# Reading the decay rows back from DRAM on all partitions in place of broadcasting them by matmul

## The chip, the cores and the metric

The kernel runs on one core of a Trainium2 chip. The metric is the device time of one execution in microseconds; the lower, the better.

## The reference

Two blocks run one after the other on a sequence of 256 positions with 1024 channels, each with two layers. A layer of the first block is a feed-forward part, a mixer of three branches (a convolution, a state-space head group, a sparse attention) and another feed-forward part, with layer norms and a modulation. A layer of the second block is a mixer of two branches (a sliding-window attention and a matrix-memory cell) and a feed-forward part.

What matters here are the two places where a decay between two positions is applied. In the state-space branch there are 16 heads in 4 groups, and for each head

```
a_cs = cumsum(a)                                # a < 0, one value for each position
seg[l, s] = exp(a_cs[l] - a_cs[s])  for l >= s, else 0
y = (C B^T * seg) (x dt)
```

In the matrix-memory branch there are 4 heads; with the input and forget gates brought to a running sum b and a running maximum, the same form appears:

```
w[l, s] = exp(b[l] - b[s] + log_i[s] - m[l]) (q_l . k_s)  for l >= s, else 0
```

In both, the exponent is a value of the column minus a value of the row, and for l >= s it is never above zero.

## The kernel before

The sequence is two tiles of 128 positions. Weights come from DRAM in pieces of 128x1024 (512 KB) on SyncE's queue; each piece is split into a high and a low part (ScalarE makes the high part at L187, VectorE the low part at L188), up to four pieces ahead. A unit is one piece with its matmuls: gemm_w (L284 to L286) does three products for each of eight channel tiles, 24 matmuls of 256 columns; gemm_x (L297 to L299) does the same with the operands exchanged, 512 columns. The program is a list of units with small actions between them. Everything that isn't a plain projection runs as a generator beside the units ("side"): after each unit step_sides advances every side by its rate, so the products of attention, convolution and heads are dealt out among the units. The convolution (conv_side, L1204) goes at a fixed number of VectorE instructions for each unit. The instruction order on each engine is fixed when the kernel is built, from the program order and the dependencies; an engine then executes its instructions in that order, and a wait holds all that stands behind it on that engine.

In the first mixer small_project computes the running sum acs for 16 heads as 16 rows of 256 positions, and to_rows turns it into columns. ssd_side takes the four groups: when a group's convolved inputs are there, one step computes the product of B and C (causal_pairs, L924 and L925, with a 0/1 mask at L928 and L929) and turns the inputs; then one step for each head calls decay and, for the head before it, decayed_sum (L934 to L936). In the second mixer mlstm_gates makes the rows and mlstm_side does the same for four heads, with causal_pairs in the same step as decay.

decay needs the row of a head on all 128 partitions, and gets it by a product: split_row has split the row into a high and a low part (tile ahl), and a one-hot column of identr picks head h and spreads it over the partitions, in two matmuls of 384 columns (L911, L912). Two further matmuls add the mask, which is minus 1e30 above the diagonal, to the two diagonal blocks (L913, L914). ScalarE then reads the sum from PSUM, adds the column value as a bias and takes the exponential (L916 with 256 elements, L917 with 128), and VectorE multiplies by the product of B and C (L918).

Of the kernel before, what the change touches and what calls it, by code (L numbers as in the profile page):

```python
# [19 lines left out]
P = 128  # L20
T = 256
# [84 lines left out]
def net_kernel(ctx, tc, a, out, dbg=None):  # L106
# [30 lines left out]
    def f(ap):  # L137
        return ap.bitcast(F32)
# [13 lines left out]
    adb = const.tile([P, DEPTH, 72], F32, name="adb")  # L152
    lncols = const.tile([P, DEPTH, 48], F32, name="lncols")
    ident = cst[:, C_ID:C_ID + P]
    identr = const.tile([P, 16], F32R, name="identr")
    V.tensor_copy(identr, ident[:, 0:16])
    ones = const.tile([P, T], F32, name="ones")
    V.memset(ones, 1.0)
    mhalf = const.tile([P, 8], F32, name="mhalf")
    V.memset(mhalf, -0.5)  # L160
    masks = const.tile([P, 4, P], BF16, name="masks")
    identb, caus_b, strict_b, tcaus_b = (masks[:, i] for i in range(4))

    def load_constants():
        late_load(lncols, a["lncol"])
        late_load(cst[:, P:], a["consts"][:, P:])
        for i, c0 in enumerate((C_ID, C_CAUS, C_STRICT, C_TCAUS)):
            V.tensor_copy(masks[:, i], cst[:, c0:c0 + P])

    def cos_t(tt, n):  # L170
# [710 lines left out]
                yield  # L881
        yield u

    def split_row(x, pp):

        t = rt("ahl", 2 * (T + P), 1, F32R).rearrange("p (a c) -> p a c", a=2)
        hi, lo = t[0:pp, 0], t[0:pp, 1]
        S.activation(hi[:, 0:T], x, AF.Copy)
        V.tensor_sub(lo[:, 0:T], x, f(hi[:, 0:T]))
        V.tensor_copy(t[0:pp, :, T:], f(t[0:pp, :, P:T]))  # L890
        return hi, lo

    def to_rows(stk):
        rows = rt("smrow", 2 * P, 1).rearrange("p (a c) -> p a c", a=2)
# [9 lines left out]
        it = iter([t[:, i * T:(i + 1) * T] for t in ts for i in range(4)])  # L904
        return lambda: next(it)

    def decay(h, hl, nh, brow, cbm):

        sp = tp_tile()[:, :T + P]
        sel = identr[0:nh, h:h + 1].to_broadcast([nh, P])  # L910
        E.matmul(sp, sel, hl[0], start=True, stop=False)  # L911
        E.matmul(sp, sel, hl[1], start=False, stop=False)  # L912
        E.matmul(sp[:, 0:P], identb, tcaus_b, start=False, stop=False)  # L913
        E.matmul(sp[:, T:T + P], identb, tcaus_b, start=False, stop=True)  # L914
        sg = rt("seg", T + P, 2)
        S.activation(sg[:, 0:T], sp[:, 0:T], AF.Exp, bias=brow[:, 0])  # L916
        S.activation(sg[:, T:], sp[:, T:], AF.Exp, bias=brow[:, 1])  # L917
        V.tensor_mul(sg, sg, cbm)  # L918
        return sg

# [124 lines left out]
    def small_project(l, st, ps):  # L1045

        pc = pcols[l]
        al = quarters()
        stk, gt = al(), al()
        G.memset(stk, 0.0)  # L1050
        it = S.activation(gt[64:112], ps[64:112, :T], AF.Tanh, scale=0.5)
        V.tensor_scalar(stk[64:112], gt[64:112], 0.5, 0.5, op0=ALU.mult, op1=ALU.add)
        x = gt[0:16]
        S.activation(x, ps[0:16, :T], AF.Identity, bias=pc[0:16, PC_DTB:PC_DTB + 1])
        for lp in softplus_log(x, 16, al):
            yield
        V.scalar_tensor_tensor(stk[0:16], x, 0.0, lp, op0=ALU.max, op1=ALU.add)
        an = small.tile([P, 1], F32, tag="an", name="an")
        with behind([it]):
            S.activation(an[0:16], pc[0:16, PC_ALG:PC_ALG + 1], AF.Exp)  # L1060
        da, acs = al()[0:16], al()[0:16]
        V.tensor_scalar(da, stk[0:16], an[0:16], -1.0, op0=ALU.mult, op1=ALU.mult)
        V.tensor_tensor_scan(acs, ones[0:16], da, 0.0, op0=ALU.mult, op1=ALU.add)
        S.activation(stk[32:48], acs, AF.Copy, scale=-1.0)
        st["hl"] = split_row(acs, 16)
        yield
        st["rows"] = to_rows(stk)
        yield
# [230 lines left out]
    def ssd_side(l, st):  # L1299
        dsk = small.tile([P, 16], F32, tag="dsk", name="dsk")  # L1300
        late_load(dsk, a["dskip"][l:l + 1].to_broadcast([P, 16]))
        yrow = row_pair()
        st["yrow"] = yrow
        for g in range(4):
            while ("xs", g) not in st:
                yield
            bcT, xg = st["bc", g], st["xs", g]
            rows, hl = st["rows"], st["hl"]
            cbm = causal_pairs(bcT[:, 0:T], bcT[:, T:])
            xdt = rt("xdt", 512, 1).rearrange("p (a h d) -> p a h d", a=2, d=HD)  # L1310
            hs, cs = slice(4 * g, 4 * g + 4), slice(g * T, (g + 1) * T)
            tp = tp_tile()
            for tt in range(2):
                for j in range(2):
                    E.transpose(tp[:, tsl(2 * tt + j)], xg[:, j * T + tt * P:j * T + (tt + 1) * P], ident)
            for tt in range(2):
                tv = tp[:, tt * T:(tt + 1) * T].rearrange("p (h d) -> p h d", d=HD)
                V.tensor_mul(xdt[:, tt], tv, bc(rows[:, tt, hs], HD))
                V.tensor_mul(yrow[tt][:, cs].rearrange("p (h d) -> p h d", d=HD), tv, bc(dsk[:, hs], HD))
            st["ssd_in"] = g + 1  # L1320
            yield
            prev = None
            for r in range(5):
                sg = decay(4 * g + r, hl, 16, rows[:, :, 32 + 4 * g + r:33 + 4 * g + r], cbm) if r < 4 else None
                if prev is not None:
                    yv = tp_tile()[:, :P].rearrange("p (a c) -> p a c", a=2)
                    decayed_sum(yv, prev, lambda tt: xdt[:, tt, r - 1])
                    for tt in range(2):
                        ys = yrow[tt][:, (4 * g + r - 1) * HD:(4 * g + r) * HD]
                        V.tensor_add(ys, ys, yv[:, tt])  # L1330
                prev = sg
                yield
            st["ssd"] = g + 1
# [236 lines left out]
    def mlstm_gates(l, st, ps):  # L1570

        gb, gf = (qcols[l][0:4, QC_GB + j:QC_GB + j + 1] for j in range(2))
        area = bt("ca", 2 * D)
        cuts = iter(range(8))

        def al():
            i = next(cuts) * T
            return area[:, i:i + T]
        stk, ix, fx = al(), al()[0:4], al()[0:4]
        G.memset(stk, 0.0)  # L1580
        S.activation(ix, ps[0:4, :T], AF.Identity, bias=gb)
        S.activation(fx, ps[0:4, T:], AF.Identity, bias=gf)
        for lp in softplus_log(fx, 4, al):
            yield

        V.scalar_tensor_tensor(lp, fx, 0.0, lp, op0=ALU.min, op1=ALU.subtract)
        bs, mx = al()[0:4], al()[0:4]
        V.tensor_tensor_scan(bs, ones[0:4], lp, 0.0, op0=ALU.mult, op1=ALU.add)
        V.tensor_sub(stk[0:4], ix, bs)
        V.tensor_tensor_scan(mx, ones[0:4], stk[0:4], 0.0, op0=ALU.mult, op1=ALU.max)  # L1590
        V.tensor_add(bs, bs, mx)
        S.activation(stk[32:36], bs, AF.Exp, scale=-1.0)
        V.tensor_scalar(mx, mx, -1.0, None, op0=ALU.mult)
        st["hl"] = split_row(mx, 4)
        yield
        yield
        st["rows"] = to_rows(stk)
        yield
# [30 lines left out]

    def mlstm_side(l, st, xm):  # L1630
        hm = row_pair()
        qk, vm, rows, hl, so = st["qk"], st["vm"], st["rows"], st["hl"], st["so"]
        prev = None
        for h in range(5):
            sg = None
            if h < 4:
                pb = (h % 2) * HD
                cbm = causal_pairs(qk[pb:pb + HD, 2 + h // 2], qk[pb:pb + HD, h // 2])
                sg = decay(h, hl, 4, rows[:, :, h:h + 1], cbm)
            if prev is not None:  # L1640
                yield
                p = h - 1
                yp = tp_tile()[:, :260].rearrange("p (a c) -> p a c", a=2)
                decayed_sum(yp, prev, lambda tt: vm[:, tt, p])
                hs = tsl(p)
                den = small.tile([P, 2], F32, tag="den", name="den")
                ss = small.tile([P, 2], F32, tag="mss", name="mss")
                sq = rt("t1", T, 4)
                S.activation(den, yp[:, :, P], AF.Abs)
                V.tensor_max(den, den, rows[:, :, 32 + p])  # L1650
                V.reciprocal(den, den)
                for tt in range(2):
                    V.tensor_scalar(hm[tt][:, hs], yp[:, tt, 0:P], den[:, tt:tt + 1], None, op0=ALU.mult)
                    S.activation(sq[:, 0:P], hm[tt][:, hs], AF.Square, accum_out=ss[:, tt:tt + 1])
                rsqrt_col(ss, ss, 1.0 / P, 1e-6)
                yield
                for tt in range(2):
                    V.scalar_tensor_tensor(hm[tt][:, hs], hm[tt][:, hs], ss[:, tt:tt + 1], so[:, tt, hs],
                                           op0=ALU.mult, op1=ALU.mult)
            prev = sg  # L1660
            yield
# [513 lines left out]
```

## Time and profile before

| what | value |
|---|---|
| median of 3 runs | 2551.43 us (2548.42 to 2554.11) |
| profiled execution | 2554.82 us, span 2552.7 us |
| TensorE, matmuls busy | 2438.5 us, 96% of the span |
| VectorE busy | 1839.7 us, 72% |
| ScalarE busy | 1344.2 us, 53% |
| mean granted TensorE clock | 0.985 of full speed |

The span runs from the first to the last instruction of one profiled execution; that execution's own time is 2.1 us longer and 3.4 us above the median of the runs. PE is TensorE, PEld its weight load, DVE is VectorE, ACT is ScalarE, SP is SyncE; an engine's name with a q is its queue of instructions (DMA issues, semaphores). Busy times count instructions that overlap once. A row of a stretch gives its limits and length, then the busy us (and instructions) of PE, PEld, DVE, ACT and POOL in it. A line number is that of the instruction or of the helper that issued it.

### The profile page before, as it was taken

The page shows a single profiled execution, that of the slowest core. Times are in us where ns is not written, and L with a number is a line of the kernel's source. Part 1 is how long each engine was busy: PE and PEld are TensorE (multiplying, and loading weights), DVE is VectorE, ACT ScalarE, POOL GpSimd, SP SyncE. Part 2 cuts the span into 40 slices and gives each one's busy share as a digit, 9 for nine tenths or more (in the row PEclk, how much of TensorE's full clock was granted, in tenths as well). Part 3 has the DMA queues.
Part 4 walks back from the last instruction along what each step waited for, and adds up shares of the span by engine and source line. Part 5 has one row for each costly group of instructions (what it writes and reads, how often), then busy time and mean ns, then how long its engine had stood idle before and what let it go on. Part 6 is the DMA issues. An engine that isn't in the chain of part 4 may idle for free.

```text
span 2552.7 us, 42530 instructions
## 1 busy us (share of the span) xinstructions
PE 2438.5 (96%) x16604; PEld 2208.8 (87%) x16604; DVE 1839.7 (72%) x3270; ACT 1344.2 (53%) x2356; POOL 69.8 (3%) x128
## 2 busy tenths in 40 slices
PE   8999999989889989989999999999899999999999
PEld 6887889889878879978898999899789898789888
DVE  7768988899786676768988996655766555656554
ACT  5444666544543444435666546545465555555554
POOL 0000000000000000000000000000100000100000
PEclk9999999999999999989999999999999999999999
DMA  9886622256868868875522357457335456436454
GB/s 332 286 301 226 217 101 92 91 171 216 270 218 279 272 205 275 273 242 173 166 67 84 117 188 231 143 189 250 119 121 185 156 187 223 134 100 223 141 187 143
DMA packets 134218, 484.73 MB, mean 190 GB/s; under 512 B 15569, under 2 KB 16129, under 8 KB 134018
## 3 DMA queue, kind: packets, MB, share of 16 engines
q1 hardware_dynamic: 133442, 480.83, 57.0%
q8 instruction: 130, 2.13, 0.3%
q10 hardware_dynamic: 576, 1.19, 0.1%
q14 instruction: 70, 0.57, 0.1%
HBM read 476.69 MB, written 5.27 MB: 189 GB/s over the span
## 4 chain that ended last, share of the span: by engine, by line
PE 61%; DMA 15%; DVE 13%; ACT 5%; issue 4%; POOL 1%; SPq 0%; ACTq 0%; DVEq 0%; POOLq 0%
PE mm L284 10%; PE mm L285 10%; PE mm L286 10%; DMA ada<-in_adaw_dram 8%; PE y L297 6%; PE y L298 6%; PE y L299 6%; DVE lo L188 4%; DVE ca L1204 2%; PE tp L989 2%; ACT hi L187 2%; DMA raw<-in_wg_dram 2%; DVE ada L492 1%; PE tp L980 1%; DMA raw<-in_wo_dram 1%
## 5 line engine op out<-in xcount | busy, mean ns | idle before, releaser
L187 ACT ACTIVATE hi<-raw 128x1024 fp32r<-128x1024 f32 (+1 forms) x676 | 712.6, 1058 | 725.1 <-PE mm L285 367.2
L188 DVE TENSOR_TENSOR lo<-raw,hi 128x1024 fp32r<-128x1024 f32 (+1 forms) x676 | 822.2, 1221 | 304.7 <-ACT hi L187 300.9
L284 PE MATMUL mm<-xTh,hi 128*128 128x256 f32 x2896 | 827.8, 286 | 10.3 <-ACT av L1222 3.0
L286 PE MATMUL mm<-xTh,lo 128*128 128x256 f32 x2896 | 824.2, 285 | 6.5 <-DVE lo L188 6.5
L285 PE MATMUL mm<-xTl,hi 128*128 128x256 f32 x2896 | 822.5, 284 | 2.4 <-DVE xTl L455 2.4
L284 PEld LDWEIGHTS mm<-xTh,hi 128*128 128x128 f32 x2896 | 551.2, 190 | 15.9 <-ACT av L1222 3.7
L286 PEld LDWEIGHTS mm<-xTh,lo 128*128 128x128 f32 x2896 | 550.8, 190 | 9.6 <-DVE lo L188 9.0
L285 PEld LDWEIGHTS mm<-xTl,hi 128*128 128x128 f32 x2896 | 550.7, 190 | 6.5 <-DVE xTl L455 3.2
L299 PE MATMUL y<-hi,q 128*128 128x512 f32 x664 | 264.5, 399 | 1.0 <-DVE q L702 1.0
L492 DVE SCALAR_TENSOR_TENSOR ada<-ada,crow 128x1024 f32<-128x1024 f32 x128 | 156.1, 1221 | 120.7 <-DMA ada<-in_adaw_dram 120.5
L297 PE MATMUL y<-hi,q 128*128 128x512 f32 x552 | 221.8, 402 | 14.2 <-ACT q L701 14.2
L298 PE MATMUL y<-lo,q 128*128 128x512 f32 x552 | 220.7, 400 | 5.0 <-DVE lo L188 5.0
L1204 DVE SCALAR_TENSOR_TENSOR ca<-av,pcol,ca 128x244 f32<-128x244 f32 (+26 forms) x480 | 207.3, 461 | 0.3
L299 PEld LDWEIGHTS y<-hi,q 128*128 128x128 f32 x664 | 126.4, 190 | 32.4 <-DVE q L702 2.0
L297 PEld LDWEIGHTS y<-hi,q 128*128 128x128 f32 x552 | 105.3, 191 | 39.0 <-ACT q L701 16.6
L298 PEld LDWEIGHTS y<-lo,q 128*128 128x128 f32 x552 | 104.9, 190 | 29.5 <-DVE lo L188 7.5
L297 PE MATMUL y<-hi,xTh 128*128 128x512 f32 (+1 forms) x288 | 114.1, 396 | 3.1 <-DVE e8b L830 1.5
L284 PE MATMUL mm<-xyh,hi 128*128 128x256 f32 x384 | 112.2, 293 | 4.2 <-ACT t2d L1366 4.2
L285 PE MATMUL mm<-xyl,hi 128*128 128x256 f32 x384 | 111.7, 291 | 4.4 <-DVE xyl L415 4.4
L286 PE MATMUL mm<-xyh,lo 128*128 128x256 f32 x384 | 111.1, 290 | 0.8 <-DVE lo L188 0.8
L299 PE MATMUL y<-hi,xTl 128*128 128x512 f32 (+1 forms) x288 | 111.1, 386 | 0.0
L298 PE MATMUL y<-lo,xTh 128*128 128x512 f32 (+1 forms) x288 | 110.7, 384 | 0.0
(492 smaller groups left out, 3730.5 us busy)
## 6 DMA issues: line engine op xcount, KB each, us to landing
ada<-in_adaw_dram SPq DMA_DIRECT2D x128, 512.0 KB, 5.2
raw<-in_ff_dram SPq DMA_DIRECT2D x128, 512.0 KB, 4.6
raw<-in_wg_dram SPq DMA_DIRECT2D x88, 512.0 KB, 5.6
raw<-in_wu_dram SPq DMA_DIRECT2D x88, 512.0 KB, 5.6
raw<-in_wd_dram SPq DMA_DIRECT2D x88, 512.0 KB, 5.4
raw<-in_wG_dram SPq DMA_DIRECT2D x48, 512.0 KB, 4.2
raw<-in_wkv_dram SPq DMA_DIRECT2D x16, 512.0 KB, 4.6
raw<-in_wval_dram SPq DMA_DIRECT2D x16, 512.0 KB, 4.3
```

The lines of the kernel that those rows point to most:

```text
L187: S.activation(hi, raw, AF.Copy)
L188: eng.tensor_tensor(lo, raw, f(hi), op=ALU.subtract)
L284: E.matmul(ps, wh[:, wk + k], xh, start=(k == 0), stop=False)
L285: E.matmul(ps, wh[:, wk + k], xl, start=False, stop=False)
L286: E.matmul(ps, wl[:, wk + k], xh, start=False, stop=(k == nk - 1))
L297: return [E.matmul(ps, xh, wh[:, kk, cs], start=first, stop=False), E.matmul(ps, xh, wl[:, kk, cs], start=False, stop=False), E.matmul(ps, ...
L298: E.matmul(ps, xh, wl[:, kk, cs], start=False, stop=False),
L299: E.matmul(ps, xl, wh[:, kk, cs], start=False, stop=last)]
L492: V.scalar_tensor_tensor(raw, raw, 1.0, crow, op0=ALU.mult, op1=ALU.mult, accum_out=col[:, k:k + 1])
L980: E.transpose(tp[:, tsl(r * nbr + b)], pr[:, r, b, tsl(kt)], ident)
L989: E.matmul(o[:, i * HD:(i + 1) * HD], pTs[kt][:, tsl(i)], vof(i % nbr, kt), start=(kt == 0), stop=(kt == tt))
L1204: V.scalar_tensor_tensor(ca[:, k, s:T], av[:, 0:T - s], caw[:, k, w:w + 1], ca[:, k, s:T], op0=ALU.mult, op1=ALU.add)
```

## The change

The one-hot, the split of the row and the four matmuls go. The rows are written to a DRAM tile by a DMA on ScalarE's queue (keep_rows, once in each layer of each mixer), and each head's row of 256 positions is read back on all 128 partitions by another DMA on that queue (decay_rows, two heads in a tile of 2 x 256, three such tiles). In the first mixer all four reads of a group are issued at the start of its step; in the second mixer all four at the start of the side, with a yield behind them. decay then works from SBUF: two Relu of the difference of column and row (on ScalarE, with scale -1 and the column as bias) make it zero where it would be negative, which is only above the diagonal, and one Exp with scale -1 over all 384 elements follows. The 0/1 mask in the product of B and C takes out what is above the diagonal. The columns change sign accordingly.

```diff
-    identr = const.tile([P, 16], F32R, name="identr")
-    V.tensor_copy(identr, ident[:, 0:16])
...
-    masks = const.tile([P, 4, P], BF16, name="masks")
-    identb, caus_b, strict_b, tcaus_b = (masks[:, i] for i in range(4))
+    masks = const.tile([P, 3, P], BF16, name="masks")
+    identb, caus_b, strict_b = (masks[:, i] for i in range(3))
...
-    def split_row(x, pp):
-
-        t = rt("ahl", 2 * (T + P), 1, F32R).rearrange("p (a c) -> p a c", a=2)
-        hi, lo = t[0:pp, 0], t[0:pp, 1]
-        S.activation(hi[:, 0:T], x, AF.Copy)
-        V.tensor_sub(lo[:, 0:T], x, f(hi[:, 0:T]))
-        V.tensor_copy(t[0:pp, :, T:], f(t[0:pp, :, P:T]))
-        return hi, lo
+    decd = [dram.tile([16, T], F32, name="decd%d" % i) for i in range(4)]
+
+    def keep_rows(st, x, i):
+        st["dec"] = decd[i][0:x.shape[0]]
+        S.dma_start(st["dec"], x)
+
+    def decay_rows(st, h):
+
+        t = rt("dec", 2 * T, 3)
+        for j in range(2):
+            S.dma_start(t[:, j * T:(j + 1) * T], st["dec"][h + j:h + j + 1].to_broadcast([P, T]))
+        st["dec", h], st["dec", h + 1] = t[:, 0:T], t[:, T:]
...
-    def decay(h, hl, nh, brow, cbm):
-
-        sp = tp_tile()[:, :T + P]
-        sel = identr[0:nh, h:h + 1].to_broadcast([nh, P])
-        E.matmul(sp, sel, hl[0], start=True, stop=False)
-        E.matmul(sp, sel, hl[1], start=False, stop=False)
-        E.matmul(sp[:, 0:P], identb, tcaus_b, start=False, stop=False)
-        E.matmul(sp[:, T:T + P], identb, tcaus_b, start=False, stop=True)
+    def decay(row, brow, cbm):
+
+
         sg = rt("seg", T + P, 2)
-        S.activation(sg[:, 0:T], sp[:, 0:T], AF.Exp, bias=brow[:, 0])
-        S.activation(sg[:, T:], sp[:, T:], AF.Exp, bias=brow[:, 1])
+        S.activation(sg[:, 0:T], row, AF.Relu, scale=-1.0, bias=brow[:, 0])
+        S.activation(sg[:, T:], row[:, P:T], AF.Relu, scale=-1.0, bias=brow[:, 1])
+        S.activation(sg, sg, AF.Exp, scale=-1.0)
         V.tensor_mul(sg, sg, cbm)
         return sg
...
-        S.activation(stk[32:48], acs, AF.Copy, scale=-1.0)
-        st["hl"] = split_row(acs, 16)
+        S.activation(stk[32:48], acs, AF.Copy)
+        keep_rows(st, acs, l)
...
+            for j in range(0, 4, 2):
+                decay_rows(st, 4 * g + j)
             cbm = causal_pairs(bcT[:, 0:T], bcT[:, T:])
...
-        V.tensor_sub(stk[0:4], ix, bs)
-        V.tensor_tensor_scan(mx, ones[0:4], stk[0:4], 0.0, op0=ALU.mult, op1=ALU.max)
+        V.tensor_sub(ix, ix, bs)
+        V.tensor_scalar(stk[0:4], ix, -1.0, None, op0=ALU.mult)
+        V.tensor_tensor_scan(mx, ones[0:4], ix, 0.0, op0=ALU.mult, op1=ALU.max)
...
-        st["hl"] = split_row(mx, 4)
+        keep_rows(st, mx, DEPTH + l)
...
+        for j in range(0, 4, 2):
+            decay_rows(st, j)
+        yield
```

## Rows read from the trace of the kernel before

**Rows 1.** The page, busy us of the engines, share of the span, instructions.
```profile
PE 2438.5 (96%) x16604; PEld 2208.8 (87%) x16604; DVE 1839.7 (72%) x3270; ACT 1344.2 (53%) x2356; POOL 69.8 (3%) x128
```

**Rows 2.** Busy time by stretch; the last columns are granted clock, DMA share, GB/s.
```profile
340.00:500.00 160.00, 159.67 (x1212) 143.78 (x1210) 130.42 (x370) 103.43 (x283) 9.98 (x26) 0.99 0.27 88
1262.00:1420.00 158.00, 157.41 (x1204) 141.52 (x1203) 129.99 (x379) 102.70 (x282) 12.67 (x28) 1.00 0.24 78
1862.00:1912.00 50.00, 49.95 (x367) 44.84 (x366) 30.02 (x84) 28.65 (x81) 1.87 (x4) 1.00 0.39 121
...
530.00:600.00 70.00, 60.29 (x452) 58.66 (x451) 66.70 (x133) 27.60 (x44) 1.42 (x2) 0.90 0.51 166
```
**Rows 3.** The chain that ended last from 340 to 500 us, by line.
```profile
by line: PE mm L284 12.3%; PE mm L286 12.2%; PE mm L285 12.1%; PE tp L989 10.5%; PE tp L980 4.9%; PE tp L1075 4.6%; PE tp L911 3.7%; PE y L946 3.5%; PE y L947 3.4%; PE tp L867 2.8%; PE y L950 2.3%; PE tp L934 2.3%; PE tp L935 2.2%; PE tp L9
```

**Rows 4.** ACT's waits from 340 to 500 us: us in total, times, longest.
```profile
ACT seg L916 <- PE tp L914: 15.1, 11, 4.1
```

**Rows 5.** Instruction groups of ACT by shape: count, busy us, mean ns, idle before.
```profile
L454 ACT ACTIVATE xTh<-t 128x256 fp32r<-128x256 f32 x72 | 28.9, 417 | 2.1 <-DVE t L446 1.1 <-DVE t L448 0.4
...
L916 ACT ACTIVATE seg<-tp,smrow 128x256 f32<-128x256 f32 x40 | 19.0, 475 | 30.6 <-PE tp L914 30.4
...
L917 ACT ACTIVATE seg<-tp,smrow 128x128 f32<-128x128 f32 x40 | 14.6, 365 | 0.0
...
L1286 ACT ACTIVATE sac<-sac 128x512 f32<-128x512 f32 x16 | 10.2, 635 | 0.3
...
L1201 ACT ACTIVATE ca<-av,pcol 128x256 f32<-128x256 f32 x16 | 8.7, 594 | 0.2
```

**Rows 6.** PE in order of time around one decay set: start us, us, instruction.
```profile
361.89 0.28 PE L284 MATMUL mm<-xTh,hi 128*128 128x256 f32 x1
362.10 0.43 PE L911 MATMUL tp<-ahl,identr 16*128 16x384 f32 x1
362.38 0.33 PE L912 MATMUL tp<-ahl,identr 16*128 16x384 f32 x1
362.64 0.23 PE L913 MATMUL tp<-masks 128*128 128x128 bf16 x1
362.71 0.22 PE L914 MATMUL tp<-masks 128*128 128x128 bf16 x1
362.74 0.37 PE L285 MATMUL mm<-xTl,hi 128*128 128x256 f32 x1
362.94 0.28 PE L286 MATMUL mm<-xTh,lo 128*128 128x256 f32 x1
363.06 0.28 PE L284 MATMUL mm<-xTh,hi 128*128 128x256 f32 x1
```

**Rows 7.** Single lines on ACT: ns min/median/max, first and last start.
```profile
L875 ACT ACT_TABLE_LOAD  x1: 1283/1283/1283, 1839.9 to 1839.9; - x1
...
L819 ACT ACTIVATE t2d<-mm x32: 575/580/598, 2000.2 to 2537.6; 128x512 f32<-128x512 f32 x32
...
L964 ACT ACTIVATE t<-y,aneg x160: 348/424/504, 355.8 to 2287.9; 128x128 f32<-128x128 f32 x80, 128x256 f32<-128x256 f32 x80
```

**Rows 8.** A DMA issue of ACT (the inputs' load): ns min/median/max, starts.
```profile
L1786 ACTq DMA_DIRECT2D row<-in_x_dram x2: 452/452/453, 1.1 to 1.6; - x2
```

**Rows 9.** Who waited for whom in the whole span: us in total, times, longest.
```profile
ACT seg L916 <- PE tp L914: 30.4, 25, 4.1
```

**Rows 10.** PE in order of time, from a group's products to its first decay.
```profile
1379.72 0.59 PE L924 MATMUL tp<-sac 128*128 128x256 f32 x2
...
1385.13 0.43 PE L911 MATMUL tp<-ahl,identr 16*128 16x384 f32 x1
```

**Rows 11.** DMA issues: count, KB each, median us to landing.
```profile
cst<-in_consts_dram ACTq DMA_DIRECT2D x1, 64.0 KB, 2.0
```

**Rows 12.** The late loads on SP's queue, L238: ns of an issue, and landing.
```profile
L238 SPq DMA_DIRECT2D row<-hd x8: 372/424/1348, 654.5 to 2323.0; - x8
...
DMA to landing us min/median/max: 5.0/6.8/9.9
```

More of the change, by code (lines that the diff above doesn't have):

```diff
@@ L166, in load_constants @@
         late_load(cst[:, P:], a["consts"][:, P:])
-        for i, c0 in enumerate((C_ID, C_CAUS, C_STRICT, C_TCAUS)):
+        for i, c0 in enumerate((C_ID, C_CAUS, C_STRICT)):
             V.tensor_copy(masks[:, i], cst[:, c0:c0 + P])
@@ L1307, in ssd_side @@
             bcT, xg = st["bc", g], st["xs", g]
-            rows, hl = st["rows"], st["hl"]
+            rows = st["rows"]
+            for j in range(0, 4, 2):
+                decay_rows(st, 4 * g + j)
             cbm = causal_pairs(bcT[:, 0:T], bcT[:, T:])
@@ L1323, in ssd_side @@
             for r in range(5):
-                sg = decay(4 * g + r, hl, 16, rows[:, :, 32 + 4 * g + r:33 + 4 * g + r], cbm) if r < 4 else None
+                h = 4 * g + r
+                sg = decay(st["dec", h], rows[:, :, 32 + h:33 + h], cbm) if r < 4 else None
                 if prev is not None:
@@ L1631, in mlstm_side @@
         hm = row_pair()
-        qk, vm, rows, hl, so = st["qk"], st["vm"], st["rows"], st["hl"], st["so"]
+        qk, vm, rows, so = st["qk"], st["vm"], st["rows"], st["so"]
+        for j in range(0, 4, 2):
+            decay_rows(st, j)
+        yield
         prev = None
@@ L1638, in mlstm_side @@
                 cbm = causal_pairs(qk[pb:pb + HD, 2 + h // 2], qk[pb:pb + HD, h // 2])
-                sg = decay(h, hl, 4, rows[:, :, h:h + 1], cbm)
+                sg = decay(st["dec", h], rows[:, :, h:h + 1], cbm)
             if prev is not None:
```

## Prediction

> **What bounds the kernel now.** I read the page's busy times first [rows 1]: TensorE (PE) is busy 96% of the span, VectorE (DVE) 72%, ScalarE (ACT) 53%. That is an average, so next I read the busy times of the stretches in which the decay products run [rows 2]. The reader is to see that PE has nothing left there: 159.67 us of 160 in the first mixer of layer 0, 157.41 of 158 in layer 1, 49.95 of 50 in the second mixer's stretch (its other layer reads the same), with DVE at 130 us of 160 and ACT at 103. The last line of that group is the stretch behind: there DVE is at 66.70 of 70 and PE at 60.29. The chain of waits in the first stretch [rows 3] runs through PE matmuls, with the first product of the change (L911) taking 3.7% of it. The list of waits [rows 4] shows the other side: ACT stood idle 15.1 us in that stretch only because the last decay product (L914) was not done. So in these stretches PE issues without a hole, and an instruction taken from it should come off the time.
>
> **What is removed from PE.** decay() runs 40 times: 16 heads in each of two layers, 4 in each of two (the count in [rows 5]). Each run has four matmuls: two of 384 columns (the row's high and low part against the one-hot) and two 128x128 masks. A PE row's own duration includes its pipeline, so I go by starts [rows 6]: L911 starts at 362.10 and the next foreign matmul at 362.74, so a set holds PE for 0.64 us. The spacing of two plain matmuls is 363.06 - 362.94 = 0.12; at the two seams it is 0.21 (361.89 to 362.10) and 0.20 (362.74 to 362.94), so the seams add up to 0.09 + 0.08 = 0.17. If the neighbours close up as plain matmuls, that goes too; if other side work stands there, it stays. 40 x 0.64 = 25.6 us is the lower bound of what PE is relieved of, 40 x 0.81 = 32.4 the upper; I take the middle of the seams, 25.6 + 3.4 = 29.0, since products of the attention fall next to a set about as often as plain ones. The PSUM tile that a set held until ACT had read it also comes free; PE has no hole there [rows 2], so no matmul waited for one and I price that at nothing.
>
> **What is added to ACT.** Before, a head costs ACT two exponentials from PSUM, 0.475 + 0.365 = 0.84 us [rows 5]. After, two Relu from SBUF of the same sizes, then one Exp over 384 elements. For the Relus the nearest rows are these same two (a pointer bias, a number as scale) as the lower bound and L1201's 0.594 (two pointers, 256 elements) as the upper; the 128 one scales to 0.365 x 0.594/0.475 = 0.46. The Exp lies between 0.417 (256 elements, L454) and 0.635 (512, L1286): 0.53. So a head costs 1.37 to 1.58 us, 0.53 to 0.74 more; over 40 heads 21 to 30 us, of which I take 24. No table load comes with it: the last one is at 1839.9 us, and Relus run from 2000.2 on in the same kernel that goes on using Exp [rows 7].
>
> Then the transfers. 4 writes of the rows and 40 reads go out on ACT's own queue; SP's and POOL's queues get nothing. Issuing costs the sequencer time: 0.45 us in the rows that ACT issues now [rows 8], so 44 x 0.45 = 20 us in all, about 1.8 at the start of a group of four heads. Together ACT gets 44 us, 17 of them in each first-mixer stretch: 16 heads at 0.6 and 16 issues at 0.45. Against it stands the 15.1 us of waiting for L914 that ends, so ACT's position in time hardly moves: 103 + 15 before, 103 + 17 after, of a stretch cut to about 150. That idle time is the cover; where it is missing, a late split of weights or a late copy of attention scores holds PE. In 25 of the 40 runs ACT waited for L914 [rows 9]; 15 of 40 had no such cover, and their share of the issue time is 15/40 x 20 = 7.5 us. I put half of it on the path, 3.7 us, and keep 0 and 20 as the bounds.
>
> The DMA engines carry it easily: 16 x 128 KB = 2.1 MB beside 88 GB/s x 160 us = 14 MB in a stretch with a share of 0.27 [rows 2].
>
> **Edits costed at nothing.** Splitting the row (one ACT and two DVE instructions, four times) goes, one DVE product per second-mixer layer comes, a one-hot copy and a mask cast at the start go; none is over the 0.475 us of L916, and DVE has 30 us of idle time in the stretch [rows 2], which hides them; uncovered they would be a gain of under 5 us. The additional yield makes mlstm_side one step longer. Counted in steps it ended with the second unit of the gate products; now the last transposes fall into the forced drain there, two units of 24 matmuls (48 x 0.12 = 5.8 us) before their first reader. Without that cover it would be a microsecond or two in each layer.
>
> **When the row must be there.** The wait for a landing sits on ACT: the first Relu of a group holds the exponentials behind it, the attention's exponentials and copies and the weight splits, and PE waits for those. In the first mixer the reads are issued in the step that computes the group's products (L924) and used in the next: the shortest of the eight intervals is 1379.72 to 1385.13, 5.4 us [rows 10]; the other seven are 5.9 to 11.5 us. In the second mixer it is one unit, 24 x 0.12 = 2.9 us. For a landing, ACT's own read of 64 KB took 2.0 us on an idle machine [rows 11]; the loads that SP issues behind others took 5.0, 6.8 and 9.9 (least, median, most) [rows 12]. The new reads have a queue to themselves, are small, and find the engines at 0.27: nearer to 2.0. I take 3, which costs the second mixer nothing that counts. The Trainium skill (DMA: Bandwidth & Descriptors, Anatomy of one DMA, for the gpsimd path) gives about 2.0 us plus the bytes at 436 GB/s, an estimate of 2.3 us here. By it no row is late and the sum stands; the 2.0 in [rows 11] agrees, those in [rows 12] don't.
>
> **Sum.** 29.0 off PE, 3.7 back from ACT: 25.3 us less. The profiled execution took 2554.8 us, so 2529.5; the median of the runs is 3.4 us below that execution, so 2526.
>
> **Rivals.**
> A, rows land late. At a landing of 6.8 us the shortest two groups lose 1.4 and 0.9, the two second-mixer groups 3.9 each: 10 us; at 9.9 also the 7.4 us interval loses 2.5, and it is 4.5 + 4.0 + 2.5 + 14 = 25, all of the gain. That speaks for 2526 + 10 = 2536. Against it: the separate queue, and weights split ahead, which let PE run on for a while. Chance 0.13.
>
> B, no change. PE is not the only engine near its end: with 10 us out of the first-mixer stretch, DVE's 130 us stand in 150. If the convolution (L1204) is what really paces the stretch, the time comes back behind it, where DVE is already the bound at 66.70 of 70 [rows 2]. Against it: its instructions are doled out per unit, and DVE has 30 us of holes in the stretch. In that case 2551. Chance 0.10.
>
> C, slower: ACT becomes the bound. All of its 24 + 20 us would then be on the path against 29.0 saved: 15 us more, 2566. It takes over where its own work plus its waits for others exceed PE's stretch: 103 + 17 + 30 = 150, so from 30 us of waiting that can't be moved. Now it waits 15.1 us for L914, which ends, and for PE's other products, which come sooner. Chance 0.11. A page speaks for this rival: the Trainium skill (Perfetto Trace Analysis, DMA Instruction — HWDGE) says that the block that makes descriptors is shared by the issuing sequencers, and that a row of an issue includes the wait for its lock. SP's longest issue of 1.348 us against a median of 0.424 [rows 12] agrees in kind. If every issue on ACT took the 1.35, that would be an estimated 59 us in place of 20.
>
> **How the numbers follow.** The forecast has 0.66; its own range is 2516 (all of the seams, nothing back from ACT, and 3 us of smaller waits gone: 2551.4 - 32.4 - 3) to 2542 (2551.4 - 29.0 + 20). With A, faster has 0.79. The bound for a difference is 0.2%, 5 us, which is about what this measurement can tell from no change; B is same, 0.10; C is slower, 0.11. The range goes from 2515 to 2550: it takes in A and half of B, and leaves out C, the other half of B and the ends.
>
> **What would show it.** Right: PE has 160 matmuls fewer, stays without holes in the two first-mixer stretches, which are each about 10 us shorter, and the stretches behind them keep their length. ACT's busy time rises by 20 to 28 us, with no more than six table loads, and an issue row stays near 0.45. Wrong by A: idle time of ACT before the Relu, released by a DMA, over 1 us on average. Wrong by B: DVE above 90% in the stretch, and the stretch behind longer by what was saved. Wrong by C: PE holes released by ACT (the weight split L187, the copies L982), issue rows on ACT of a microsecond. What would undo all of it is another order of the instructions: it is made when the kernel is built, and every engine's could shift with the instructions that are gone.

## The result and the profile after

The changed kernel takes 2534.46 us in the median (2529.52 to 2535.35) beside 2551.78 us (2548.42 to 2554.11) for the kernel before on the same chip. The ratio is 0.9923 with an interval of 0.9906 to 0.9940, and a second measurement (e10 below) gives 0.9921 [0.9906, 0.9937]. So the change gains 17 us by the medians, 20 us by the ratios; 25.3 us were forecast. The profiled execution took 2529.52 us, 4.9 below its median, with a span of 2527.7 us; the one of before lay 3.4 above its own. So the two spans lie 25.0 us apart, 5 to 8 more than the measured gain.

First the page's busy times of the kernel after, with the columns of [rows 1].

```profile
PE 2406.0 (95%) x16444; PEld 2190.9 (87%) x16444; DVE 1835.2 (73%) x3262; ACT 1359.8 (54%) x2392; POOL 67.4 (3%) x128
```

The 160 matmuls are gone, and PE is busy 32.5 us less. ACT is busy 15.6 us more. Next the ACT groups of decay in the kernel after, by shape, which stand in place of L916 and L917 in [rows 5].

```profile
L916 ACT ACTIVATE seg<-seg 128x384 f32<-128x384 f32 x40 | 20.8, 521 | 0.5
L914 ACT ACTIVATE seg<-dec,smrow 128x256 f32<-128x256 f32 x40 | 20.3, 509 | 6.1 <-PE tp L935 5.8
L915 ACT ACTIVATE seg<-dec,smrow 128x128 f32<-128x128 f32 x40 | 16.0, 399 | 0.0
```

A head costs 0.521 + 0.509 + 0.399 = 1.43 us there, 0.59 more than before, inside the forecast 1.37 to 1.58. The groups grew by 57.1 - 33.6 = 23.5 us; ACT's busy time rose by less because it counts overlapping instructions once, and because four copies of 0.42 us that split the rows are gone. The 30.4 us that ACT waited for the mask product [rows 9] are gone: before the first Relu 5.8 us are left, for another product, and none for a DMA.

The reads themselves, as the single line L893 of the kernel after shows them (issue in ns, and from issue to landing):

```profile
L893 ACTq DMA_DIRECT2D dec<-decd x40: 326/327/1745, 333.0 to 2209.3; - x40
...
DMA to landing us min/median/max: 3.0/3.3/5.1
```

An issue takes 0.327 us in the median, less than the 0.452 in [rows 8], and one of the 40 took 1.745; a landing takes 3.3.

Then the stretches of the kernel after (columns as in [rows 2]): the first-mixer stretch of each layer up to a like place in PE's work as before, and behind it the part up to the norm of the convolution (L1245).

```profile
340.00:486.00 146.00, 143.44 (x1123) 134.07 (x1122) 121.31 (x347) 106.83 (x285) 11.10 (x26) 0.99 0.32 101
...
1245.00:1392.00 147.00, 144.54 (x1141) 135.08 (x1140) 122.44 (x353) 108.44 (x291) 10.07 (x27) 1.00 0.31 94
...
1392.00:1515.00 123.00, 117.55 (x920) 112.80 (x920) 115.50 (x230) 60.74 (x99) 3.15 (x5) 0.99 0.47 153
486.00:616.00 130.00, 119.72 (x913) 113.87 (x912) 126.18 (x256) 60.70 (x102) 5.42 (x6) 0.97 0.55 178
```

The same two parts behind the stretch in the kernel before:

```profile
1420.00:1533.00 113.00, 111.34 (x893) 107.86 (x891) 107.65 (x204) 59.82 (x96) 3.70 (x5) 1.00 0.50 164
497.00:630.00 133.00, 122.98 (x928) 117.95 (x927) 125.80 (x251) 60.92 (x103) 4.13 (x5) 0.95 0.53 173
```

Both stretches are 11 us shorter by these limits: from 157 us (340 to 497) to 146 in layer 0, and from 158 [rows 2] to 147 in layer 1. The limits don't fall on one and the same matmul. Counted in the trace from ACT's table load (the mark used below), PE starts the 720th matmul of a weight piece 13.0 us sooner in layer 0 (194.5 to 181.5) and 8.6 us sooner in layer 1 (191.6 to 183.0). But in layer 1 the part behind is 10 us longer, 113 to 123, and DVE has 7.85 us more to do in it at 94% busy. In layer 0 that part is 3 us shorter. So one of the two layers gave its gain back. The granted clock of that part was 1.00 before and 0.99 after in layer 1, and 0.95 and 0.97 in layer 0, so a lower clock is not what took it. What DVE carried over is seen in its groups, in the stretch of layer 1 and then in the part behind. Before, from 1233 to 1420 us and from 1420 to 1533:

```profile
L188 DVE TENSOR_TENSOR lo<-raw,hi 128x1024 fp32r<-128x1024 f32 x33 | 40.0, 1216 | 0.5 <-ACT hi L187 0.4
L1204 DVE SCALAR_TENSOR_TENSOR ca<-av,pcol,ca 128x249 f32<-128x249 f32 (+22 forms) x68 | 30.1, 455 | 0.0
...
L1204 DVE SCALAR_TENSOR_TENSOR ca<-av,pcol,ca 128x243 f32<-128x243 f32 (+25 forms) x119 | 50.5, 464 | 0.0
L188 DVE TENSOR_TENSOR lo<-raw,hi 128x1024 fp32r<-128x1024 f32 x36 | 43.8, 1218 | 0.9 <-ACT hi L187 0.9
```

After, from 1215 to 1392 and from 1392 to 1515:

```profile
L186 DVE TENSOR_TENSOR lo<-raw,hi 128x1024 fp32r<-128x1024 f32 x32 | 38.9, 1217 | 0.0
L1203 DVE SCALAR_TENSOR_TENSOR ca<-av,pcol,ca 128x226 f32<-128x226 f32 (+29 forms) x55 | 24.6, 461 | 0.0
...
L1203 DVE SCALAR_TENSOR_TENSOR ca<-av,pcol,ca 128x248 f32<-128x248 f32 (+22 forms) x133 | 56.0, 462 | 0.0
L186 DVE TENSOR_TENSOR lo<-raw,hi 128x1024 fp32r<-128x1024 f32 x37 | 45.0, 1215 | 1.2 <-ACT hi L185 1.2
```

A tap is one VectorE instruction of the convolution, one shifted product. DVE has 187 or 188 of them to do here in either kernel. In the stretch it did 68 before and 55 after, so 14 taps more, 5.5 us, are left for the part behind, and one split of a weight with them. (In layer 0 the stretch held 54 taps before and 53 after.)

### The profile page after: what moved, and what is told of

The parts are those of the page before. It is cut to its first block, busy times and chain, and to the rows that moved or that the text cites. A ratio compares the mean times of both kernels' runs of the same rounds, so it can differ in the third digit from the quotient of the medians.

```text
span 2527.7 us, 42258 instructions
## 1 busy us (share of the span) xinstructions
PE 2406.0 (95%) x16444; PEld 2190.9 (87%) x16444; DVE 1835.2 (73%) x3262; ACT 1359.8 (54%) x2392; POOL 67.4 (3%) x128
## 5 line engine op out<-in xcount | busy, mean ns | idle before, releaser
L186 DVE TENSOR_TENSOR lo<-raw,hi 128x1024 fp32r<-128x1024 f32 (+1 forms) x676 | 822.1, 1221 | 294.1 <-ACT hi L185 292.1
L1203 DVE SCALAR_TENSOR_TENSOR ca<-av,pcol,ca 128x226 f32<-128x226 f32 (+26 forms) x480 | 207.2, 462 | 0.3
```

What stands on the lines that cost most here:

```text
L186: eng.tensor_tensor(lo, raw, f(hi), op=ALU.subtract)
L1203: V.scalar_tensor_tensor(ca[:, k, s:T], av[:, 0:T - s], caw[:, k, w:w + 1], ca[:, k, s:T], op0=ALU.mult, op1=ALU.add)
```

## The layers as a yardstick

For the experiments one reading is repeated: the start of ACT's table load in each first mixer (L1060 before, L1059 after) and the start of the first and the last normalizing of the convolution's output (L1246, L1245). The lines give the first and the last start, in layer 0 and layer 1. Before:

```profile
L1060 ACT ACT_TABLE_LOAD  x2: 1283/1283/1283, 312.8 to 1233.5; - x2
L1246 ACT ACTIVATE row<-tp,nb,rstd x8: 769/774/780, 629.6 to 1532.6; 128x512 f32<-128x512 f32 x8
```

After:

```profile
L1059 ACT ACT_TABLE_LOAD  x2: 1283/1283/1283, 310.4 to 1215.1; - x2
L1245 ACT ACTIVATE row<-tp,nb,rstd x8: 762/770/777, 616.1 to 1514.8; 128x512 f32<-128x512 f32 x8
```

So layer 0 takes 629.6 - 312.8 = 316.8 us before and 616.1 - 310.4 = 305.7 after, layer 1 takes 299.1 and 299.7.

How early the normalizing starts doesn't tell how far PE has come with its other work. So a second reading stands beside it, the whole layer: from the same table load to the next one, which stands before the first activation of the feed-forward part behind the mixer (L813 before, L811 after). Before, after, and for e8 and e4 further down:

```profile
L813 ACT ACT_TABLE_LOAD  x2: 1283/1283/1283, 731.3 to 1618.9; - x2
L811 ACT ACT_TABLE_LOAD  x2: 1283/1283/1283, 716.3 to 1600.6; - x2
L813 ACT ACT_TABLE_LOAD  x2: 1283/1283/1283, 719.9 to 1612.3; - x2
L811 ACT ACT_TABLE_LOAD  x2: 1283/1283/1283, 716.7 to 1588.8; - x2
```

The same differences for every run, from one profiled execution of each (us; "between" goes from the first normalizing to the table load of layer 1, and "rest" from the last normalizing to the end of the span; "rest" holds the second mixers):

| kernel | layer 0 | between | layer 1 | rest | whole layer 0 | whole layer 1 |
|---|---|---|---|---|---|---|
| before | 316.8 | 603.9 | 299.1 | 1020.1 | 418.5 | 385.4 |
| after | 305.7 | 599.0 | 299.7 | 1012.9 | 405.9 | 385.5 |
| after, again (e10) | 303.7 | 597.9 | 299.7 | 1014.8 | 403.6 | 387.5 |
| after + matmuls (e1) | 316.1 | 600.4 | 300.2 | 1023.0 | 418.0 | 387.6 |
| before, half the taps (e3) | 289.1 | 603.5 | 288.3 | 1032.1 | 399.0 | 387.3 |
| after, half the taps (e3) | 275.6 | 601.5 | 273.8 | 1025.5 | 385.9 | 371.5 |
| after + matmuls, half the taps (e11) | 287.2 | 600.3 | 284.4 | 1030.0 | 395.6 | 382.4 |
| before, product on POOL (e8) | 306.6 | 606.4 | 289.3 | 1030.6 | 408.0 | 387.4 |
| after, product on POOL (e4) | 302.3 | 597.3 | 288.1 | 1016.1 | 403.1 | 375.6 |

The two profiles of the changed kernel differ by up to 2.3 us in a part; smaller differences are not read.

The busy times of the whole of layer 1, before and after (columns as in [rows 2]), show where the removed matmuls went:

```profile
1233.50:1618.90 385.40, 377.19 (x2876) 350.09 (x2876) 327.30 (x722) 234.04 (x493) 19.76 (x38) 1.00 0.42 138
1215.10:1600.60 385.50, 369.08 (x2812) 346.58 (x2811) 326.61 (x720) 241.11 (x508) 15.65 (x38) 0.99 0.45 143
```

PE has 64 matmuls fewer and is busy 8 us less, and the layer is as long as before: PE's idle time doubled, from 8.2 to 16.4 us. PE's lead of 8.6 us at the 720th matmul of a weight piece was 4.5 at the 1080th and 2.0 at the 1296th.

## Experiments

**e1: the matmuls issued again, for nobody.**

```diff
-    def decay(row, brow, cbm):
+    def decay(row, brow, cbm, hl, h):
+        sp, nh = tp_tile()[:, :T + P], hl.shape[0]
+        sel, hl = identr[0:nh, h:h + 1].to_broadcast([nh, P]), bm(hl, 3)
+        E.matmul(sp, sel, hl, start=True, stop=False)
+        E.matmul(sp, sel, hl, start=False, stop=False)
+        E.matmul(sp[:, 0:P], identb, caus_b, start=False, stop=False)
+        E.matmul(sp[:, T:T + P], identb, caus_b, start=False, stop=True)
...
```

A copy on ACT for each set of rows, four in all, makes the operand hl.

> The changed kernel with a decay set's four matmuls issued again (same sizes, operands that are at hand, into a PSUM tile that nothing reads); rows, guard and transfers stay as changed. If the gain is the time of these matmuls on PE, all of it goes: 2550 to 2556 us, at most a few us over before for what ACT does more. If it came from another order of the instructions, or from ACT no longer waiting for PE, most of it stays: 2534 to 2540.

Measured: 2559.40 us (before 2551.96), 1.0023 [1.0009, 1.0036]. The gain is gone, and a little more. Against the changed kernel (0.9923) the four matmuls cost 1.0%, 25.5 us. In the profile 10.4 us of that lie in layer 0 and 0.5 in layer 1 (12.1 and 2.1 by the whole layers). Its profiled execution took 2551.21 us, 8 less than its median, so the profile doesn't show where its slower executions lose time.

**e2: the transfers on SP's queue.**

```diff
-        S.dma_start(st["dec"], x)
+        nc.sync.dma_start(st["dec"], x)
...
-            S.dma_start(t[:, j * T:(j + 1) * T], st["dec"][h + j:h + j + 1].to_broadcast([P, T]))
+            nc.sync.dma_start(t[:, j * T:(j + 1) * T], st["dec"][h + j:h + j + 1].to_broadcast([P, T]))
```

> The changed kernel with its 44 transfers issued by SP in place of ACT. If the issue time on ACT (40 x 0.33 us) lies in ACT's idle time, taking it away is worth nothing: 2530 to 2537, unless SP, whose issues stand behind waits for weight buffers, brings the rows late; then slower, 2540 to 2550, with ACT waiting for a DMA before the Relu. If the issues on ACT are what the gain is short of the forecast: 2526 or less.

Measured: 2532.59 us, 0.9920 [0.9906, 0.9935]: no different from the change. ACT's issues cost nothing that shows. Behind SP's other loads four reads came late, by 6.6 us in all, as the line of the first Relu shows in the list of who it waited for, and that cost nothing either.

**e3: half the taps, in both kernels.** The same edit before and after; it takes 83 us of busy time from DVE and touches nothing of the decay.

```diff
-                    V.scalar_tensor_tensor(ca[:, k, s:T], av[:, 0:T - s], caw[:, k, w:w + 1], ca[:, k, s:T],
-                                           op0=ALU.mult, op1=ALU.add)
+                    if w % 2:
+                        V.scalar_tensor_tensor(ca[:, k, s:T], av[:, 0:T - s], caw[:, k, w:w + 1], ca[:, k, s:T],
+                                               op0=ALU.mult, op1=ALU.add)
```

> The kernel before with every second tap of the convolution (L1204) left out, 240 of 480 VectorE instructions, 55 us in each first mixer. It is one half of a pair with the next run. The stretch behind the attention, where VectorE was at 66.7 of 70 us, should get shorter: 2515 to 2540.

> The changed kernel with the same taps left out. If VectorE takes back behind the stretch what PE saves in it (17 us of some 27 reach the end), the pair differs by the whole saving of PE, 24 to 30 us. If the shortfall lies with ACT or with the order, the pair differs by the same 17 us as the whole kernels, 14 to 20.

Measured: 2529.17 us, 0.9902 [0.9888, 0.9916] before, and 2495.07 us, 0.9773 [0.9760, 0.9785] after. The pair differs by 34.1 us, where the full kernels differ by 17 to 20; that is above the 24 to 30 expected. The lines of the yardstick, before with half the taps:

```profile
L1060 ACT ACT_TABLE_LOAD  x2: 1283/1283/1283, 315.5 to 1208.1; - x2
...
L1247 ACT ACTIVATE row<-tp,nb,rstd x8: 771/774/780, 604.6 to 1496.4; 128x512 f32<-128x512 f32 x8
```

After with half the taps:

```profile
L1059 ACT ACT_TABLE_LOAD  x2: 1283/1283/1283, 315.2 to 1192.3; - x2
...
L1246 ACT ACTIVATE row<-tp,nb,rstd x8: 770/774/780, 590.8 to 1466.1; 128x512 f32<-128x512 f32 x8
```

Layer 1 now keeps its gain: 288.3 to 273.8, 14.5 us, where it kept nothing with all taps; by the whole layer it is 387.3 to 371.5. What took layer 1's gain back was DVE's work. In the kernel before, half the taps make the whole of layer 1 no shorter (385.4 to 387.3): there PE's work, 377 us of it, held the layer.

**e11: the matmuls again, with half the taps.** Both edits above together; it tells whether the 34 us are the matmuls.

> The changed kernel with the four matmuls issued again into a PSUM tile that nothing reads, and with every second tap of the convolution left out (so its output is not that of the reference). It stands beside three runs: the matmuls issued again with all taps (1.0023 of before), and every second tap left out in the kernel before (0.9902) and in the changed one (0.9773). Theory: the removed matmuls are what the whole difference of 34 us between the last two is made of, and what ACT and the DMAs got costs nothing where DVE is relieved; then this kernel is at 0.990 to 0.991 of before, 2527 to 2529 us. First rival: the additions cost some 6 us of their own, as the 1.0023 would say, with or without the taps; then it is at 0.9925 or above, 2533 us. Second rival: the matmuls are worth no more than the 25 us that they cost when they were issued again with all taps, and the rest of the 34 is something else; then it is at 0.987, 2519 us.

Measured: 2524.05 us (before 2554.39 on that chip), 0.9885 [0.9865, 0.9905]. The matmuls cost 0.9885 - 0.9773 = 1.12%, 28.6 us, of the 1.29% that the e3 pair differs by. The first rival (0.9925) lies outside the interval: with DVE relieved, what the change added to ACT and the DMA queues shows no cost. Of the theory's 0.990 to 0.991 the lower end lies within it, and the second rival's 0.987 too, so what the last 4 us are is not told apart. By the whole layers e11 is 3.4 and 4.9 us shorter than the kernel before with half the taps, which has as many matmuls; why is not shown. The yardstick's lines are clearer:

```profile
L1068 ACT ACT_TABLE_LOAD  x2: 1283/1283/1283, 313.4 to 1200.9; - x2
...
L1255 ACT ACTIVATE row<-tp,nb,rstd x8: 768/774/780, 600.6 to 1485.3; 128x512 f32<-128x512 f32 x8
```

The same 64 matmuls of layer 1 cost 284.4 - 273.8 = 10.6 us here, and 300.2 - 299.7 = 0.5 us with all taps (10.9 and 2.1 by the whole layer). In layer 0 it is 11.6 and 10.4.

**e4 and e8: the product with C B^T on POOL.** One line, in the changed kernel (e4) and in the kernel before (e8). POOL is GpSimd, and it is 3% busy.

```diff
-        V.tensor_mul(sg, sg, cbm)
+        G.tensor_tensor(sg, sg, cbm, op=ALU.mult)
```

> The changed kernel with the last product of a decay (L917, 40 of 0.55 us, 22 us of VectorE) given to GpSimd, which is idle 97% of the span. If VectorE is what takes back the saving behind the stretch, part of the 22 us comes off: 2522 to 2531. If VectorE has slack wherever it counts: 2532 to 2537. If the product on GpSimd comes too late for decayed_sum, or slows VectorE: above 2540.

> The kernel before with the last product of a decay (L918) given to GpSimd, the same 22 us of VectorE as in the run on the changed kernel, where it was worth 0.66% (0.9857 against 0.9923). If VectorE became the taker only through the change, PE still holds the stretch here and the product's move is worth much less: 0.996 to 1.001 of before. If VectorE's time is worth as much in either kernel: 0.992 to 0.995.

Measured: e4 2519.59 us (before 2556.31 on its chip), 0.9857 [0.9839, 0.9875]; e8 2543.45 (before 2552.95), 0.9965 [0.9952, 0.9979]. e4 is faster than both kernels, 0.9857/0.9923 = 0.9934 of the changed one, 17 us. Layer 1 shortens by 11.6 us (299.7 to 288.1) for 16 products of 0.548 us, 8.8 us, that DVE no longer does in it; by the whole layer it is 9.9 (385.5 to 375.6). In e8 the normalizing in layer 1 comes 9.8 us sooner too, but "rest" grows by 10.5, and the whole layer takes 387.4 us where it took 385.4. So in the kernel before, DVE's relief alone is worth nothing in layer 1; the removed matmuls alone are worth nothing there either (385.5); both together bring 10 us. PE and DVE had about equally long ways through that layer, and each change alone leaves the other one. e8's time lies in the range expected for the case that PE still holds the stretch. In layer 0 either change pays alone, 12.6 us for the matmuls and 10.5 for the product, and both bring 15.4.

The price on POOL, and what it did to DVE, in e4's groups:

```profile
L917 POOL TENSOR_TENSOR seg<-seg,cbm 128x384 f32<-128x384 f32 x40 | 49.9, 1253 | 159.5 <-ACT seg L916 80.1 <-DVE cbm L928 65.6 <-PE mm L283 5.7
...
L186 DVE TENSOR_TENSOR lo<-raw,hi 128x1024 fp32r<-128x1024 f32 (+1 forms) x676 | 825.0, 1225 | 300.6 <-ACT hi L185 296.9 <-issue 2.1
L1203 DVE SCALAR_TENSOR_TENSOR ca<-av,pcol,ca 128x244 f32<-128x244 f32 (+26 forms) x480 | 212.7, 472 | 0.3
```

In the changed kernel the last two groups take 822.1 and 207.2 us, so they are 2.9 + 5.5 = 8.4 us longer in e4, of the 21.9 that DVE hands over. The price is not fixed: in e8, with the same product on POOL, the two groups grow by 2.5 us only (822.2 to 822.8 and 207.3 to 209.2).

**e9: a second product on POOL.** e4, and the state-space branch's gating product as well.

```diff
-        V.tensor_mul(ys, ys, t)
+        G.tensor_tensor(ys, ys, t, op=ALU.mult)
```

> The changed kernel with the decay's last product and also the gate's product of ssm_gate (8 of 128x512, 0.69 us each on VectorE) on GpSimd. If VectorE is still what limits behind the stretch, a little more than the first move: 0.981 to 0.985 of before. If GpSimd's longer products now stand in front of readers: 0.986 to 0.990.

Measured: 2521.05 us, 0.9879 [0.9861, 0.9897], no better than e4, and in the range expected for products on POOL that stand in front of their readers. Whether that is the reason, or that DVE has time to spare where this product stands, isn't shown.

**e5: the convolution dealt out faster.** If taps are left over, deal more of them beside the heads.

```diff
-            rate(st["conv_gen"], 1.5)
+            rate(st["conv_gen"], 2.5)
```

> The changed kernel with 2.5 convolution steps for each unit in place of 1.5 during the attention, so that more of VectorE's work lies in the stretch and less behind it. If the place of this work is what costs (VectorE has holes in the stretch and none behind it): 2520 to 2531. If VectorE has by now no room in the stretch, the work delays the attention and it is the same or slower: 2533 to 2545.

Measured: 2538.31 us, 0.9935 [0.9913, 0.9957]: no gain, in the range expected for a DVE without room in the stretch. By the same yardstick layer 1 shortens by 5.5 us to 294.2, and "rest" grows by 8.7; the whole layer takes 389.9, longer than the 385.5 and 387.5 of the changed kernel.

**e6: without the Exp.** ACT's added work shrinks by 20.8 us.

```diff
-        S.activation(sg, sg, AF.Exp, scale=-1.0)
```

> The changed kernel with the Exp over 384 elements left out (40 of 0.52 us, 21 us of ScalarE); the heads multiply with the guarded exponent itself. If what the change adds to ScalarE lies in its idle time: 2531 to 2537. If it is on the path, up to all of it: 2514 to 2529.

Measured: 2534.50 us, 0.9916 [0.9898, 0.9934], the same as with it. The Exp on ACT is hidden.

**e7: the rows read in the step that uses them.**

```diff
-            for j in range(0, 4, 2):
-                decay_rows(st, 4 * g + j)
...
+                if r in (0, 2):
+                    decay_rows(st, h)
```

The second mixer's reads move in the same way, and its additional yield goes.

> The changed kernel with each pair of rows read in the step that uses it, without the step between. The landing takes 3.3 us (median), and 20 pairs could each hold ScalarE that long, 66 us at most. If a late row is what the early reads avoid, ScalarE waits for the DMA before the Relu and some of it reaches PE: 2540 to 2570. If weights split ahead and the order of the build hide it anyway: 2532 to 2539.

Measured: 2531.91 us, 0.9906 [0.9891, 0.9921]: nothing lost. The line of the reads shows that ACT waited for them twice, 1.8 us in all; the instruction order made when the kernel is built still puts the issues ahead of their use, 32 of the 40 by over 20 us.

**e10: the change once more**, unaltered, beside e9 on its chip.

> The changed kernel once more, on the same chip as these two: 0.990 to 0.994 of before, so that the two can be read against it.

Measured: 2531.71 us, 0.9921 [0.9906, 0.9937]. Its layer 1 takes 299.7 us as in the first profile, and 387.5 as a whole; what layer 1 gave back is no accident of one execution.

## Why the prediction was right, and where it was not

The forecast was 2526 us within 2515 to 2550, faster; it came to 2534.5, faster.

- **PE's share was right** as the time that the matmuls hold PE. 29.0 us were forecast, between 25.6 and 32.4. Where DVE doesn't hold the layers, the matmuls put back cost 28.6 us, give or take 6 (e11). With all taps they cost 25.5 (e1), but e1's profile finds hardly any of that in layer 1, and some 6 us of it lie above the kernel before and are not explained.
- **The stretches** were to be 10 us shorter each: 11 and 11 by the limits taken, 13.0 and 8.6 by the 720th matmul. **That the stretches behind them keep their length** is the step that failed, for layer 1. There 10 us came back (113 to 123 us), because DVE had used the stretch to do 68 taps and now did 55. This is rival B's mechanism, a convolution that paces the part behind, in one of the two layers. It paced it only once the matmuls were gone: before, PE held the layer as a whole (e3, e8), and DVE was close behind (385.5 us without the matmuls, 385.4 with them). PE's lead became idle time, 16.4 us in place of 8.2. I had priced it as all or nothing at 0.10 of chance and asked for DVE above 90% in the stretch as its sign; DVE was at 83% there (122.44 of 147 us). The sign was in the part behind: 107.65 of 113 us in layer 1 before, 95% busy. I had read that only for layer 0, at 66.70 of 70 [rows 2], and layer 0 is the layer that kept its gain. Why its stretch held 53 taps as before in less time, the runs do not settle.
- **The term "back from ACT", 3.7 us, was put on the wrong engine.** Neither the issues nor the Exp taken off ACT makes the kernel faster (e2, e6). What came back is some 10 us of layer 1, by DVE. That the total missed by only 5 to 8 us is in part luck: some 4 us are gained between the mixers (603.9 to 599.0), where no decay product runs, and the whole of layer 0 gained 12.6 and 14.9 us in the two profiles, where 16 sets at 0.73 make 11.7. e1 has most of the gain between the mixers too (600.4), so that part isn't the matmuls; its cause stays open.
- **The sizes on ACT** were right: 1.43 us for a head, six table loads as before, issues at 0.33 in place of 0.45. Rival C is out by e2 and e6; of its signs a single issue above a microsecond was seen, 1.745 us.
- **Rival A is out.** A landing takes 3.3 us where I took 3 and the estimate beside it was 2.3, and even reads in the step of use lose nothing (e7).
- **The second mixers** gave 7.2 us in "rest" and 5.3 in the second profile (8 sets at 0.73 would be 5.8).

What stays open: by its ratio e1 is 6 us (2 to 9) above the kernel before though it has the same number and sizes of matmuls, and its profile doesn't show where.

## What to carry to other kernels

An engine that is full in a stretch makes time saved on it real in that stretch; whether it stays real is decided in the stretch behind, by the engine that fills up there. So read the part behind at every place where the change acts, and count what the second engine does beside the removed work, because that work will have to go somewhere. Where two engines have about equally long ways through a layer, relief of either one alone can pay nothing, and a trial of one alone tells little about the other. When the second engine takes the gain back, move some of its work to an idle one: here one product on POOL brought 17 us more, and 9 in the kernel before.

## What the hardware showed

- A DVE instruction can get longer beside POOL's products: in e4 the combining of attention's output (L1117), which took at most 287 ns in the changed kernel, took 1133 ns at its longest. The product itself took a median of 1018 ns on POOL and 550 ns on DVE. The Trainium skill (SBUF — State Buffer, Who interferes with whom) says that a DVE instruction with two inputs in SBUF contends with a GpSimd instruction that reads SBUF, that the pair of ports they share is an exclusive lock, and that the order of issue decides who is blocked. The trace of e4 agrees: the longest one started at 438.94 us, 0.03 us behind a product on POOL (438.91 to 439.92), and ended 0.15 us behind that product's end.
- A broadcast read of 128 KB to 128 partitions landed 3.0 to 5.1 us after its issue from ACT's queue (median 3.3), and 2.9 to 4.8 from SP's (3.7, e2).
- Relu with a column as bias took 509 ns for 256 elements from SBUF, Exp 475 ns for the same size from PSUM [rows 5].
